# The up projection of a transformer layer by Strassen's seven block products, in a phase of its own

## The chip, the core and the metric

The kernel runs on one core of one Trainium2 chip. A core has TensorE (PE, matmuls into PSUM; PEld is its weight load), VectorE (DVE), ScalarE (ACT), GpSimd (POOL) and SyncE (SP), which here issues every DMA. The metric is the device time of one execution in microseconds, as the median of several runs; lower is better.

## The reference: what is computed

One layer of a hybrid backbone over 1024 latent tokens and 128 context tokens, in float32. A mixer (bidirectional mLSTM and attention) comes first, then a feed-forward block with a normalisation behind it. Only the second half matters here:

```python
x = layer_norm(ALPHA * x + g1 * mix, ln1_g, ln1_b)
h = x * (1 + sc2) + sh2
ff = jnp.square(jax.nn.relu(h @ w_up)) @ w_down
x = layer_norm(ALPHA * x + g2 * ff, ln2_g, ln2_b)
```

`h` is 1152 x 1024 (both token groups together), `w_up` 1024 x 4096, `w_down` 4096 x 1024.

## The kernel before, in words

Float32 products are made of three matmuls. `split` (L69) writes a rounded copy `hi` (ScalarE) and the rest `lo = src - hi` (VectorE); `mm3` (L73) issues hi x hi, hi x lo and lo x hi into one PSUM bank. Every operand of a large matmul goes through `split` first.

The work runs in four stages: projections and mLSTM, attention, branch projections with merge and output projection, feed-forward. Tokens stand in nine groups of 128 (`NT`), three of which make a block of 384 (`TB`, `NTB` = 3). A scheduler of the compiler sets the order on each engine from the program's order and the dependencies; engines take their rows strictly in that order and wait by semaphores. Buffers come from pools with a tag and a number of copies; a tile waits until its copy is free.

At the end of stage 3, for each token group, the output projection (`g3`) is followed by residual, `layer_norm` (VectorE statistics, GpSimd for the root and the gain, VectorE for the bias), a store of `x1` to DRAM, and `modulate2`: eight transposes on TensorE, eight scale-and-shift steps (four on VectorE, four on ScalarE), and a split into `h2T`, which stays in SBUF. The last group's `modulate2` is issued from within the first up block (the `mid` argument of `up`).

The feed-forward takes 16 blocks of 256 hidden units (`NFB`). `up(fb)` (L1111) multiplies a block of `w_up` with all tokens: three token blocks, two halves of the hidden units, eight steps of the contraction, three matmuls each, 144 of 384 columns. ScalarE's Relu, VectorE's square and a split follow. `down(fb)` (L1131) adds the block's share of the output: nine token groups, two halves of the columns, two steps, three matmuls, 108 of 512 columns; VectorE adds each result to `acc` (L1143). The loop puts `up(fb + 1)` ahead of `down(fb)`. The last two blocks go down together (`last`), with the final residual and `finish` (second normalisation and output) behind each group. `residual(s)` (L1158) adds the gate and `x1` to `acc`; it is spread over the last `up`, its `x1` tile has one buffer.

## Time and profile before

| quantity | value |
|---|---|
| median of 3 runs | 2476.15 us (2475.36 to 2480.89) |
| profiled execution, first to last instruction | 2469.1 us |
| feed-forward, from the first up matmul (1651.5) to the end | 817.6 us |
| TensorE busy, share of the span | 97% |
| VectorE, ScalarE, GpSimd busy | 57%, 34%, 13% |
| mean granted TensorE clock | 0.990 |
| moved by DMA | 264.8 MB, 107 GB/s |

The profile has the span of the profiled execution, not what lies around it; the median is 7.05 us above the span. In rows of groups stand the line, the engine, the operation, output and inputs by the program's names, the shape and the count, then busy time and the mean of one in ns, then the idle time before and what ended it. In rows in order of time stand the start, the length, the engine, the line, the names, and in brackets an idle time before with what ended it. A matmul's recorded length overlaps its neighbours'. In the view of stretches, each engine's busy time and count stand in the order PE, PEld, DVE, ACT, POOL, then clock, DMA share and GB/s.

### The profile page before, as it was taken

The numbers are of one execution on the slowest core, as the hardware profiler recorded it, in microseconds if no ns is written. First come the engines' busy times: TensorE is split into PE (matmuls) and PEld (weight loads), VectorE is DVE, ScalarE is ACT, GpSimd is POOL, SyncE is SP. The second block draws the span as 40 slices with busy tenths as digits, with TensorE's granted clock in tenths as the row PEclk, the third lists the DMA queues.
The fourth block names the chain that finished last, engine by engine and source line by source line (L and its number), as shares of the span: only waits on it lengthen the run. The fifth ranks groups of instructions, "written<-read, shape, count | busy, mean of one in ns | idle before, by whom it ended". The sixth has DMA issues, their size and how long they took to land. (4 is left out here: it accounts for less than half of the span.)

```text
span 2469.1 us, 35511 instructions
## 1 busy us (share of the span) xinstructions
PE 2387.7 (97%) x13485; PEld 2163.7 (88%) x13485; DVE 1399.7 (57%) x2625; ACT 843.8 (34%) x1844; POOL 312.3 (13%) x514
## 2 busy tenths in 40 slices
PE   6999998999999899899999999999999999999997
PEld 4888887788899899889999999888999899989985
DVE  5645635645654464378787345674445444544488
ACT  3323423534433243266666333132221122212221
POOL 1001100211110010134442000230000000000004
PEclk9999999999999999999999999999999999999998
DMA  7264447445654642520001655241111111111131
GB/s 266 87 206 152 148 120 198 138 125 146 196 165 145 183 148 95 104 72 17 16 16 58 216 188 189 93 141 35 52 35 52 35 52 35 51 35 52 35 120 77
DMA packets 211162, 264.77 MB, mean 107 GB/s; under 512 B 23760, under 2 KB 157984, under 8 KB 210992
## 3 DMA queue, kind: packets, MB, share of 16 engines
q1 hardware_dynamic: 210992, 262.51, 34.7%
q8 instruction: 106, 1.74, 0.3%
q14 instruction: 64, 0.52, 0.1%
HBM read 197.23 MB, written 65.21 MB: 106 GB/s over the span
## 5 line engine op out<-in xcount | busy, mean ns | idle before, releaser
L76 PE MATMUL g<-th,wh 128*128 128x384 f32 x1088 | 373.5, 343 | 8.7 <-DVE fm L246 8.7
L78 PE MATMUL g<-th,wl 128*128 128x384 f32 x1088 | 368.3, 338 | 0.0
L77 PE MATMUL g<-tl,wh 128*128 128x384 f32 x1088 | 366.7, 337 | 0.0
L70 ACT ACTIVATE wh<-raw 128x1024 fp32r<-128x1024 f32 x148 | 154.9, 1058 | 405.8 <-PE d L78 289.4
L76 PE MATMUL u<-th,wh 128*128 128x384 f32 x768 | 256.8, 335 | 0.8 <-ACT th L70 0.8
L77 PE MATMUL u<-tl,wh 128*128 128x384 f32 x768 | 256.7, 334 | 0.6 <-DVE tl L71 0.6
L78 PE MATMUL u<-th,wl 128*128 128x384 f32 x768 | 256.7, 334 | 0.0
L76 PE MATMUL g<-wh,th 128*128 128x512 f32 x600 | 241.1, 402 | 0.0
L77 PE MATMUL g<-wl,th 128*128 128x512 f32 x600 | 236.1, 394 | 0.7 <-DVE wl L71 0.7
L78 PE MATMUL g<-wh,tl 128*128 128x512 f32 x600 | 236.5, 394 | 0.0
L1143 DVE TENSOR_TENSOR acc<-acc,d 128x512 f32<-128x512 f32 x234 | 159.4, 687 | 119.6 <-PE d L78 119.6
L77 PE MATMUL d<-wl,ah 128*128 128x512 f32 x576 | 224.6, 390 | 2.3 <-DVE wl L71 2.3
L76 PE MATMUL d<-wh,ah 128*128 128x512 f32 x576 | 224.4, 390 | 1.8 <-DVE r L1146 1.6
L78 PE MATMUL d<-wh,al 128*128 128x512 f32 x576 | 224.4, 390 | 0.0
L76 PEld LDWEIGHTS g<-th,wh 128*128 128x128 f32 x1088 | 206.3, 190 | 17.5 <-DVE fm L246 9.0
L71 DVE TENSOR_TENSOR wl<-raw,wh 128x1024 fp32r<-128x1024 f32 x148 | 180.8, 1230 | 71.2 <-ACT wh L70 70.6
L78 PEld LDWEIGHTS g<-th,wl 128*128 128x128 f32 x1088 | 206.1, 189 | 0.4 <-issue 0.4
L77 PEld LDWEIGHTS g<-tl,wh 128*128 128x128 f32 x1088 | 206.4, 190 | 0.1
L1123 DVE TENSOR_TENSOR r<-r 128x384 f32<-128x384 f32 x96 | 53.5, 558 | 166.4 <-ACT r L1122 166.3
L76 PEld LDWEIGHTS u<-th,wh 128*128 128x128 f32 x768 | 144.1, 188 | 1.7 <-ACT th L70 1.1
L77 PEld LDWEIGHTS u<-tl,wh 128*128 128x128 f32 x768 | 144.2, 188 | 1.5 <-DVE tl L71 1.0
L78 PEld LDWEIGHTS u<-th,wl 128*128 128x128 f32 x768 | 144.1, 188 | 0.0
(307 smaller groups left out, 4675.4 us busy)
## 6 DMA issues: line engine op xcount, KB each, us to landing
raw<-in_w_in_dram SPq DMA_DIRECT2D x44, 512.0 KB
kvt<-kvd SPq DMA_DIRECT2D x64, 257.0 KB
raw<-in_w_mod_dram SPq DMA_DIRECT2D x32, 512.0 KB
raw<-in_w_up_dram SPq DMA_DIRECT2D x32, 512.0 KB
raw<-in_w_down_dram SPq DMA_DIRECT2D x32, 512.0 KB
kvd<-kvs SPq DMA_DIRECT2D x36, 257.0 KB
uw<-ud SPq DMA_DIRECT2D x72, 128.0 KB
bs<-st SPq DMA_DIRECT2D x32, 258.0 KB
```

What stands on the lines that cost most here:

```text
L70: nc.scalar.activation(out=hi, in_=src, func=AF.Copy)
L71: nc.vector.tensor_tensor(out=lo, in0=src, in1=f(hi), op=ALU.subtract)
L76: nc.tensor.matmul(out, lhsT=ah, rhs=bh, start=start and i == 0, stop=False)
L77: nc.tensor.matmul(out, lhsT=ah, rhs=bl, start=False, stop=False)
L78: nc.tensor.matmul(out, lhsT=al, rhs=bh, start=False, stop=stop and i == n - 1)
L1123: nc.vector.tensor_tensor(out=r, in0=r, in1=r, op=ALU.mult)
L1143: nc.vector.tensor_tensor(out=acc[:, s, cs], in0=acc[:, s, cs], in1=g[:], op=ALU.add)
```

## The change

The up projection is computed by Strassen's scheme (in Winograd's form) on 2 x 2 blocks: the contraction is halved into 512 and 512, the hidden units of a block into 128 and 128, and the tokens of a part into two halves. Two parts (`SUB`): 512 tokens with halves of 256, and 640 with halves of 320. Each of the seven products is four contraction steps of three matmuls, 12 matmuls of 256 or 320 columns, 84 per part and block. The activation operands (`act_forms`: four sums and differences, seven splits per part) are made once and stay; the weight operands are made for every block (`up_forms`: four combinations on GpSimd, L1177, and seven splits). The products add up in three PSUM tiles per part (`x`, `y`, `z`), and `evac` combines them by VectorE, with relu and square, into `ao`, which is stored to DRAM (`ffd`).

So that it fits, the feed-forward is two phases. `modulate2` stores `h2` to DRAM (`h2d`) in place of splitting it; the pools of the stages before are closed; the first four entries of `up_run` take block 0 and 1 for part 0, then 0 and 1 for part 1, with `act_forms` spread over them; the other 14 take both parts in turn. Then the up phase's pools are closed, and the down phase loads each block's activations from `ffd`, splits them and its weights (`down_load`), and multiplies as before. `residual` for all groups is issued after block 13's `down`.

```diff
+SUB = ((0, 256), (512, 320))
     def modulate2(s):
-        if s % 3 == 0:
-            h2T.append(t_alloc())
         hf = dt_([128, KT, 128], "m", 8)
         modulate(hf, s, x1s[s], sc2p, 24, t3)
-        o = (s % 3) * 128
-        split(h2T[s // 3][0][:, :, o:o + 128], h2T[s // 3][1][:, :, o:o + 128], hf[:])
+        store(h2d[s][:], hf[:])
...
+    modulate2(NS)
     st3.close()
+    stw.close()
+    st3r.close()
...
+    ORDER = ("a11", "s2", "a12", "s3", "s1", "a22", "s4")
...
+    def act_forms(i, pieces):
...
+        form("a11", b11)
+        t1 = ft([128, 4, 320], "bt")[:, :, 0:n]
+        sub(t1, b12, b11)
+        sub(b11, b22, t1)
+        form("s2", b11)
+        yield
+        form("a12", b21)
+        yield
+        sub(b12, b22, b12)
+        form("s3", b12)
+        yield
+        form("s1", t1)
+        yield
+        sub(b11, b21, b11)
+        form("a22", b11)
+        yield
+        form("s4", b22)
+        yield
...
+    def up_forms(raw):
...
+        def comb(tag, x, y, op):
+            t = ft([128, 4, 128], tag)
+            nc.gpsimd.tensor_tensor(out=t[:], in0=x, in1=y, op=op)
+            return t[:]
+
+        def form(src):
+            hi, lo = ft([128, 4, 128], "uh", 3, F32R), ft([128, 4, 128], "ul", 3, F32R)
+            split(hi[:], lo[:], src)
+            return hi, lo
...
+    def evac(st, j, fb, i):
...
+        if j == 0:
+            nc.scalar.activation(out=u("u1"), in_=X[:], func=AF.Copy)
+            st["a"] = ft([128, 2, 640], "ao", 2)[:, :, 0:2 * n]
+        elif j == 1:
+            tsum(u("u2"), st["u1"][:], Y[:])
...
+            nc.vector.scalar_tensor_tensor(out=dst, in0=dst, scalar=0.0, in1=dst, op0=ALU.max, op1=ALU.mult)
+            if j == 6:
+                store(ffd[fb][i][:], st["a"])
...
+            for j, nm in enumerate(ORDER):
+                for i in subs:
...
+                    for k in range(4):
+                        for a_, b_ in ((wh, bh), (wh, bl), (wl, bh)):
+                            nc.tensor.matmul(o, lhsT=a_[:, k, :], rhs=b_[:, k, :], start=first,
+                                             stop=k == 3 and b_ is bh and a_ is wl, skip_group_check=True)
...
+    up_run([(0, (0,), hook0), (1, (0,), None), (0, (1,), hook1), (1, (1,), None)] + [(fb, (0, 1), None) for fb in range(2, NFB)])
+    st4.close()
...
+    def down_load(fb):
+        ws = []
+        ar = et([128, 2, 1152], "ar", 2)
...
+            load(ar[:, :, o:o + 2 * n], ffd[fb][i][:])
...
+            ah, al = et([128, 1152], "ah", 5, F32R), et([128, 1152], "al", 5, F32R)
+            split(ah[:], al[:], ar[:, m, :])
+            wh, wl = et([128, D], "wh", 5, F32R), et([128, D], "wl", 5, F32R)
+            split(wh[:], wl[:], raw[:])
...
+    nxt = down_load(0)
     for fb in range(NFB - 2):
-        nxt = up(fb + 1)
-        down([fb], [a], False)
-        a = nxt
+        cur, nxt = nxt, down_load(fb + 1)
+        down(cur, fb == 0, False)
...
+    for s in range(NT):
+        residual(s)
+    down(nxt + down_load(NFB - 1), False, True)
```

How the rows of an engine's queue move is shown at three places. The first is SP's queue at the change of stage; `x1d` and `h2d` are the DRAM copies of a token group's normalised and modulated values, `raw` and `ur` weight tiles, `b00` to `b11` the four quarters of part 0's activations. Before, the first weights of the up projection (`in_w_up`) stood ahead of the first group's store:

```order
L64 DMA raw_16908<-in_w_out_dram 128x2x512
L64 DMA raw_16914<-in_w_out_dram 128x2x512
L64 DMA raw_17740<-in_w_up_dram 128x4x256
L64 DMA raw_17746<-in_w_up_dram 128x4x256
L64 DMA m_16996<-in_x_sample_dram 128x1024
L67 DMA x1d0_268<-m_16926 128x1024
```

Now:

```order
L70 DMA h2d7_284<-m_17738 128x1024
L70 DMA x1d8_276<-m_17668 128x1024
L70 DMA h2d8_285<-m_17758 128x1024
L67 DMA b00_17792<-h2d0_277 128x4x128
L67 DMA b00_17792<-h2d1_278 128x4x128
L67 DMA b01_17795<-h2d2_279 128x4x128
L67 DMA b01_17795<-h2d3_280 128x4x128
L67 DMA b10_17798<-h2d0_277 128x4x128
L67 DMA b10_17798<-h2d1_278 128x4x128
L67 DMA b11_17801<-h2d2_279 128x4x128
L67 DMA b11_17801<-h2d3_280 128x4x128
L67 DMA ur_17819<-in_w_up_dram 128x4x256
```

The first up weights moved from before the last groups' stores to the ninth place behind the last of them.

The second place is VectorE's queue in the first up block (`r` and `al` were its squares and splits; `fa110l` and the like are the low parts of part 0's activation operands, `ul` those of the weights, `u2` a sum of products). Before:

```order
L1123 TENSOR_TENSOR r_17890<-r_17890 128x384
L71 TENSOR_TENSOR al_17753<-r_17890,ah_17752 128x384
L1123 TENSOR_TENSOR r_17920<-r_17920 128x384
L71 TENSOR_TENSOR al_17753<-r_17920,ah_17752 128x384
L71 TENSOR_TENSOR wl_18158<-raw_18155,wh_18157 128x1024
```

Now:

```order
L74 TENSOR_TENSOR fs20l_17812<-b00_17792,fs20h_17811 128x1024
L74 TENSOR_TENSOR fs30l_17850<-b01_17795,fs30h_17849 128x1024
L74 TENSOR_TENSOR ul_17834<-s2_17825,uh_17833 128x512
L74 TENSOR_TENSOR ul_17840<-ur_17821,uh_17839 128x512
L74 TENSOR_TENSOR ul_17869<-s3_17831,uh_17868 128x512
L74 TENSOR_TENSOR fs10l_17874<-bt_17808,fs10h_17873 128x1024
L1201 TENSOR_TENSOR u2_0_17889<-u1_0_17865,y_17872 128x256
L74 TENSOR_TENSOR ul_17892<-s1_17823,uh_17891 128x512
L1140 TENSOR_TENSOR b00_17792<-b10_17798,b00_17792 128x4x256
L74 TENSOR_TENSOR ul_17915<-ur_17821,uh_17914 128x512
```

The activations' operands stand among the weights' and the sums, ahead of what the later products of the same entry need.

The third place is VectorE's queue ahead of the last phase (`acc` the running output, `x1` the reloaded residual; `r` at L1123 the squares of the last up block, at L1146 before and L1329 now the first evacuation of the last phase). Before:

```order
L71 TENSOR_TENSOR al_22874<-r_23018,ah_22873 128x384
L1168 SCALAR_TENSOR_TENSOR acc_17960<-x1_23027,acc_17960 128x1024
L1123 TENSOR_TENSOR r_23056<-r_23056 128x384
L71 TENSOR_TENSOR al_22874<-r_23056,ah_22873 128x384
L71 TENSOR_TENSOR wl_23113<-raw_23110,wh_23112 128x1024
L1168 SCALAR_TENSOR_TENSOR acc_17960<-x1_23061,acc_17960 128x1024
L71 TENSOR_TENSOR wl_23119<-raw_23116,wh_23118 128x1024
```

Now:

```order
L1351 SCALAR_TENSOR_TENSOR acc_21878<-x1_24260,acc_21878 128x1024
L1350 TENSOR_TENSOR acc_21878<-acc_21878,g20_24244 128x1024 x2
L1350 TENSOR_TENSOR acc_21878<-acc_21878,g21_24246 128x1024
L74 TENSOR_TENSOR al_24290<-ar_24284,ah_24289 128x1152
L1351 SCALAR_TENSOR_TENSOR acc_21878<-x1_24264,acc_21878 128x1024
L74 TENSOR_TENSOR wl_24294<-dw_24287,wh_24293 128x1024
L74 TENSOR_TENSOR al_24300<-ar_24284,ah_24299 128x1152
L74 TENSOR_TENSOR wl_24304<-dw_24297,wh_24303 128x1024
L1351 SCALAR_TENSOR_TENSOR acc_21878<-x1_24268,acc_21878 128x1024
L1329 TENSOR_TENSOR r_24321<-d4_24308,g20_24244 128x512
```

The residual steps moved from between the squares of the last up block to between block 13's evacuations and the last phase, with block 15's splits among them; three of them come later still.

More of the change, by code (lines that the diff above doesn't have):

```diff
@@ L1130, in down, with act_load @@
[L1130 to L1131 removed]
+    ORDER = ("a11", "s2", "a12", "s3", "s1", "a22", "s4")
+    acts = {}
+    def act_load(i):
+        o, n = SUB[i]
+        out = []
+        for kh in range(2):
+            for th in range(2):
+                t = ft([128, 4, 320], f"b{kh}{th}")[:, :, 0:n]
+                c = o + th * n
+                while c < o + th * n + n:
+                    w = min(128 - c % 128, o + th * n + n - c)
+                    load(t[:, :, c - o - th * n:c - o - th * n + w], h2d[c // 128][:, 4 * kh:4 * kh + 4, c % 128:c % 128 + w])
+                    c += w
+                out.append(t)
+        return out
@@ new lines, in hybrid_step_kernel, with up_load @@
+    wuv = kview(w_up)
+    def up_load(fb):
+        out = []
+        for kh in range(2):
+            t = ft([128, 4, 256], "ur", 3)
+            load(t[:], wuv[:, 4 * kh:4 * kh + 4, 256 * fb:256 * fb + 256])
+            out.append(t)
+        return out
+    def up_forms(raw):
+        a11, a21 = raw[0][:, :, 0:128], raw[0][:, :, 128:256]
+        a12, a22 = raw[1][:, :, 0:128], raw[1][:, :, 128:256]
+        def comb(tag, x, y, op):
[4 more added lines that the diff above has]
+            hi, lo = ft([128, 4, 128], "uh", 3, F32R), ft([128, 4, 128], "ul", 3, F32R)
+            split(hi[:], lo[:], src)
+            return hi, lo
+        s1 = comb("s1", a21, a22, ALU.add)
+        s2 = comb("s2", s1, a11, ALU.subtract)
+        yield form(a11)
+        s3 = comb("s3", a11, a21, ALU.subtract)
+        yield form(s2)
+        s4 = comb("s4", a12, s2, ALU.subtract)
+        yield form(a12)
+        yield form(s3)
+        yield form(s1)
+        yield form(a22)
+        yield form(s4)
@@ L1132, in down @@
+    def down(ws, first, last):
         for s in range(NT):
```

157 lines of the change are left out of this document (103 added, 54 removed).

## The prediction

> **What bounds the kernel now.** I read the page's head and slices first, then the stretches of 100 us over the feed-forward, then single matmuls in order of time.
>
> ```profile
> span 2469.1 us, 35511 instructions
> PE 2387.7 (97%) x13485; PEld 2163.7 (88%) x13485; DVE 1399.7 (57%) x2625; ACT 843.8 (34%) x1844; POOL 312.3 (13%) x514
> ```
>
> ```profile
> 1700.00:1800.00 100.00, 100.00 (x511) 91.50 (x510) 46.95 (x68) 20.68 (x33) 0.00 (x0) 1.00 0.14 43
> 2300.00:2400.00 100.00, 99.45 (x506) 90.44 (x504) 64.31 (x85) 19.81 (x33) 0.00 (x0) 1.00 0.28 95
> ```
>
> The columns of the second view are stretch, PE, PEld, DVE, ACT and POOL busy, clock, DMA share, GB/s. TensorE never rests in the feed-forward, at full clock; VectorE is half idle, GpSimd empty. So a saving in matmul time counts here, and so does every wait that the change opens on TensorE. What one matmul costs is its start-to-start distance, not its recorded length (matmuls overlap):
>
> ```profile
> 1439.94 0.33 PE L76 MATMUL g<-th,wh 128*128 128x384 f32 x1
> 1459.87 0.33 PE L77 MATMUL g<-xl,wh 128*128 128x384 f32 x1
> ...
> 1704.46 0.39 PE L76 MATMUL d<-wh,ah 128*128 128x512 f32 x1
> 1728.76 0.39 PE L78 MATMUL d<-wh,al 128*128 128x512 f32 x1
> ...
> 1344.13 0.28 PE L76 MATMUL pv<-ph,vh 128*128 128x256 f32 x1
> 1346.74 0.28 PE L78 MATMUL pv<-ph,vl 128*128 128x256 f32 x1
> ```
>
> Between the rows lie 115, 107 and 23 steps: 0.1733 us for 384 columns, 0.227 for 512, 0.1135 for 256. A block of 256 hidden units costs 16 x 9 = 144 matmuls of 384 columns up, 24.96 us, and 108 of 512 down, 24.5 us.
>
> **What the change saves.** Up, a block is now seven products of 12 matmuls for each token part, 84 of 256 columns and 84 of 320. No row has 320: between the rows of 256 and 384, by length, it is 0.1435 us; its ends are 0.140 (the 256 row's excess of 7 ns over 256 columns at the 0.417 ns per column between 384 and 512) and 0.147 (the 384 row's excess of 13 ns). A block takes 84 x (0.1135 + 0.1435) = 21.6, with a little at the starts 21.7 us (21.3 to 22.0). Over 16 blocks that saves 16 x 3.26 = 52 us. Is a steady block still TensorE's? VectorE's steps:
>
> ```profile
> 2379.62 2.36 DVE L71 TENSOR_TENSOR wl<-raw,wh 128x1024 fp32r<-128x1024 f32 x2
> 1664.32 1.02 DVE L1123 TENSOR_TENSOR r<-r 128x384 f32<-128x384 f32 x2
> L1181 POOL TENSOR_TENSOR acc<-acc,l 128x1024 f32<-128x1024 f32 x8 | 20.6, 2572 | 16.7 <-DVE acc L1180 14.5 <-PE d L78 2.1
> ```
>
> The second of two adds 1.14 us at 1024 and 0.46 at 384; by that line 512 takes 0.6, 1280 1.41, 256 and 320 0.33 and 0.40. A block has seven weight splits of 512 (4.2), ten sums of the products, five a part (3.7), and four squares of 256 to 640 (2.1): 10 us of 21.7. GpSimd's four combinations of 512 (L1177) are half of the L1181 row each, 1.2 us (the eight of that row have 2.57 at 1024, 2.40 where nothing came between, below), 4.8 us together. Even one after the other the two engines fit. A weight operand has three buffers, so it can be made as soon as the product three before it has ended, and is needed two products (6.2 us) later; ScalarE's half and VectorE's half of it take 1.2 us together. So I take no stall in the 14 steady blocks: 14 x 21.7 = 304 us. What I cost at nothing besides: the activations' way through DRAM, 1.2 MB out in a block up, 1.2 MB and 1 MB of weights in a block down, lies beside 21.7 and 24.5 us of matmuls; at the 371 GB/s of a row below 2.2 MB are 6 us, with 3 fixed, and if that cover were gone each down block would pay these 9. ScalarE's squares of the first product (two of 256 and 320) lie beside the same matmuls, since it is 21% busy in the 1700 row.
>
> **What it adds: four places where TensorE waits.** First, the start. Before, the last row group's normalisation ran beside the first up matmuls:
>
> ```profile
> 1651.55 0.42 PE L76 MATMUL u<-th,wh 128*128 128x384 f32 x1
> ...
> 1652.71 0.68 DVE L1091 TENSOR_TENSOR m<-g,m 128x512 f32<-128x512 f32 x1
> 1657.79 0.81 DVE L1056 TENSOR_SCALAR m<-m,bmv,brs 128x1024 f32<-128x1024 f32 x1 [0.72 <-POOL brs L1048]
> 1662.04 1.23 DVE L1058 TENSOR_TENSOR m<-m 128x1024 f32<-128x1024 f32 x1 [2.30 <-POOL m L1057]
> ...
> 1658.74 3.26 POOL L1057 TENSOR_TENSOR m<-m 128x1024 f32<-128x1024 f32 x1 [0.98 <-issue]
> ...
> 1654.99 1.49 ACT L197 ACTIVATE m<-t,modT,sc2p 128x128 f32<-128x128 f32 x4
> ```
>
> Now all loads of the new phase stand on SP's queue behind the store of that last group, though the first part needs only groups 0 to 3: eight loads of activations and three of weights are queued there, ScalarE's first split waits for the first of them, VectorE for ScalarE, TensorE for both. The chain ended at 1663.3; it loses two weight splits (2.1) and GpSimd's wait beside a third (0.85), so 1660.3. Transposes (1.0), four L197-like steps (1.5) and the issue bring the first load to 1663.3. Ahead of the first weights lie 1 MB of stores and 2.1 MB of loads, then 0.5 MB:
>
> ```profile
> 9.00:11.00 2.00, 1.87 (x8) 0.14 (x8) 0.00 (x0) 0.00 (x0) 0.00 (x0) 1.00 1.06 371
> 30.00:34.00 4.00, 3.01 (x11) 2.69 (x9) 0.69 (x1) 0.63 (x1) 0.00 (x0) 0.68 1.04 412
> 34.00:38.00 4.00, 2.80 (x20) 2.12 (x20) 3.23 (x9) 1.71 (x3) 0.00 (x0) 1.00 1.03 386
> ```
>
> At 371 GB/s 3.6 MB take 9.7 us, so weights at about 1673, split at 1673.7: 22.2 us without up matmuls (18 if the stores are through earlier, 27 with a slower transfer).
>
> Second, the ramp, the first four entries of the new loop (blocks 0 and 1, each part alone), 43.2 us of TensorE work. VectorE must make all activation operands in it: 12 steps of 1.14 us for part 0 and 12 of 1.41 for part 1. When the first product starts five of part 0's are through; before the third entry's last operand come 8.0 + 16.9 + 21 weight splits (12.6) + evacuations (2 x 2.6 and 0.8) = 43.5 us, then two products (3.4) and the fourth entry (12.1): 59 us, the ramp ends at 1732.7. GpSimd's 12 combinations of these entries add up to 14.4 us, if they shut VectorE out:
>
> ```profile
> 2418.84 2.40 POOL L1181 TENSOR_TENSOR acc<-acc,l 128x1024 f32<-128x1024 f32 x1 [2.31 <-DVE acc L1180]
> ...
> 2409.62 0.69 DVE L1147 TENSOR_TENSOR acc<-acc,r 128x512 f32<-128x512 f32 x1
> 2419.40 2.39 DVE L1147 TENSOR_TENSOR acc<-acc,r 128x512 f32<-128x512 f32 x1
> 2418.68 0.68 DVE L1146 TENSOR_TENSOR r<-d,g 128x512 f32<-128x512 f32 x1
> ```
>
> The same sum of 512 takes 0.69 us alone and 2.39 beside GpSimd, ending just after it; one with a PSUM operand took its usual 0.68. The ramp's splits all read SBUF twice, so I lean to the upper end, 1747, and take 1745: 71.3 us. The Trainium skill, "SBUF — State Buffer", section "Who interferes with whom", says that a two-SBUF-input VectorE operation and a GpSimd operation that reads SBUF take one port pair in turn, the later waiting in full. By that rule the ramp ends at 1747, without it at 1733; the L1147 rows agree with it.
>
> Third, the handover. The first loads of the down phase stand on SP behind the last store and need the up phase's memory. Two 320-wide evacuations (1.0), then a store and 1.2 MB of activations. What a load costs beyond its bytes:
>
> ```profile
> 2390.09 1.22 DVE L1168 SCALAR_TENSOR_TENSOR acc<-x,acc 128x1024 f32<-128x1024 f32 x1 [2.53 <-DMA x<-x1d]
> 2395.69 1.23 DVE L1168 SCALAR_TENSOR_TENSOR acc<-x,acc 128x1024 f32<-128x1024 f32 x1 [2.75 <-DMA x<-x1d]
> ```
>
> From the end of the one (2391.3) to the start of the other lies one reload of 0.5 MB: 4.4 us, 1.4 of it bytes, 3.0 fixed. So 1.0 + 3.0 + 3.1, then ScalarE's three splits (3.4) and one subtraction (1.3) before the second matmul, 12 us; the clock falls in such a pause (0.68 over 30 to 34 us in the row above, where matmuls came after idling), about 1.5 us more: 13.5 (10 to 17).
>
> Fourth, the end. The down blocks stay 24.5 us, 14 of them 342.7. The residuals, once beside the last up block, now run with block 13 and after it: after block 13's last evacuation VectorE's queue has six steps of them (6.8), the two pairs of splits of block 15 (4.8) and a wait for the single x1 buffer (about 1: a reload of 4.4 us against the 3.6 of steps between) before the first of the last 18 evacuations, 12.6 us after block 13. Behind that wait stand the evacuations, and behind the splits TensorE, whose last phase sums blocks 14 and 15 in one bank: it gets through six matmuls and stops. Three more (3.7 us) fall within the last phase, which is VectorE's already:
>
> ```profile
> 2403.68 0.69 DVE L1146 TENSOR_TENSOR r<-d,g 128x512 f32<-128x512 f32 x1 [0.35 <-PE d L78]
> ...
> 2464.57 1.29 DVE L1181 TENSOR_TENSOR acc<-acc,l 128x512 f32<-128x512 f32 x2
> ```
>
> From 2403.68 to the span's end are 65.4 us; now 69.1.
>
> **The sum.** 1651.5 + 22.2 = 1673.7; + 71.3 = 1745.0; + 304 = 2049; + 13.5 + 342.7 = 2405.2; + 12.6 + 69.1 = 2486.9, against the span of 2469.1. The median of the runs, 2476.15, is 7.05 above that span; I leave this as it is: **2494 us**, 0.7% slower. The saving of 52 is spent on start, ramp excess (28), handover and end.
>
> **Rivals.** A, faster: the splits keep pace and TensorE sets the ramp, 43.2 instead of 71.3: 2465.7. Below 48.7 us of ramp the change is a gain. Its idle half on VectorE speaks for it, the sum of 43.5 us before the third entry's last operand, without any wait, against it. B, no change: narrow matmuls lose their fixed part. At the bare 0.417 ns per column of the 384 and 512 rows, 256 and 320 columns take 0.107 and 0.133 us, a block 20.2, the 14 steady ones 21 us less: 2473. The 256 row of 0.1135 speaks against. The Trainium skill, "TensorE: Matmul & The Clock Gate", section "Back-to-back issue gap", has a rule near it, columns over 2.4 GHz plus 2.5 ns. By that rule 512 columns take 0.216 us, and the trace, 0.227, does not follow it; with it the forecast would be about 2479. C, slower: GpSimd's turn lands on an operand that TensorE waits for in each steady block, 1.2 us x 14: 2510.6. The 6 us of lead speak against. D, slower: with pauses between its products TensorE stays at half clock through the ramp's fourth entry too, 12 us more: 2506. The 0.68 row speaks for it, the next row, with the clock at 1.00 though TensorE was busy in 2.8 of 4 us, against it. E, the products are not cheaper in time, each as long as one of 384 columns: 14 x 7.4 = 104 us more, 2598; the 256 row excludes nearly all of it.
>
> **How the numbers follow.** My forecast has 0.57, with its own range 2480 to 2506 (ramp 1733 to 1749, start, handover and end by their ends); A 0.08, B 0.10, C 0.12, D 0.11, E 0.02. The range of 2472 to 2514 leaves out A and E and a tail on either side. A measurement tells 0.2%, 5 us, from no change: below 2471.2 lies A and a thread of the forecast's low tail, 0.11; to 2481.1 B and a part of that tail, 0.13; above it 0.76.
>
> **What would show it.** In the changed profile the first up matmul stands about 1674, the steady blocks at 21.7 us with TensorE full, the down phase's first matmul about 13 us after the last product, and a pause after its fourteenth block. A ramp under 50 us, or steady blocks over 22.5 us, would make the working wrong; a start before 1665 would mean that the queue order did not hold.

## The result, and the profile after

The changed kernel takes 2514.11 us (median of 4 runs, 2513.26 to 2515.53) against 2475.76 of the kernel before in the same comparison (2471.35 to 2480.89): 1.0153 times as long, with a 95% interval of 1.0139 to 1.0167, or 38.4 us. Slower, as forecast, but by twice the 18 us that were forecast, and 0.1 us above the range's upper end. The profiled execution has a span of 2511.4 us, and its own time is 2513.26.

Page of the changed kernel, its head:

```profile
span 2511.4 us, 37272 instructions
PE 2366.3 (94%) x13869; PEld 2136.4 (85%) x13869; DVE 1525.5 (61%) x2796; ACT 868.4 (35%) x1879; POOL 409.5 (16%) x586
```

Against before, TensorE is busy for 21.4 us less in a span that is 42.3 us longer, and VectorE for 125.8 us more. The time went into waits of TensorE. Where they lie is read from single rows in order of time: the last matmul of the output projection, the first of the up phase, the start of its fifth entry (block 2), a steady block, the last of the up phase, and the stops of the down phase.

```profile
1653.91 0.40 PE L81 MATMUL g<-wh,tl 128*128 128x512 f32 x1
1680.27 0.58 PE L1260 MATMUL x<-fa110h,uh 128*128 128x256 f32 x1 [15.33 <-ACT uh L73]
1754.16 0.28 PE L1260 MATMUL x<-fa110h,uh 128*128 128x256 f32 x1
...
1821.36 0.28 PE L1260 MATMUL x<-fa110h,uh 128*128 128x256 f32 x1
1822.79 0.31 PE L1260 MATMUL x<-fa111h,uh 128*128 128x320 f32 x1
1824.56 0.28 PE L1260 MATMUL y<-fs20h,uh 128*128 128x256 f32 x1
1843.76 0.28 PE L1260 MATMUL x<-fa110h,uh 128*128 128x256 f32 x1
...
2067.61 0.31 PE L1260 MATMUL z<-fs41h,ul 128*128 128x320 f32 x1
2079.14 1.22 PE L79 MATMUL d<-wh,ah 128*128 128x512 f32 x2 [11.22 <-ACT wh L73]
2089.67 0.50 PE L79 MATMUL d<-wh,ah 128*128 128x512 f32 x1 [1.63 <-DVE acc L1324]
2434.75 0.80 PE L80 MATMUL d<-wl,ah 128*128 128x512 f32 x1 [2.51 <-DVE wl L74]
```

Twelve matmuls of 256 columns go from 1821.36 to 1822.79, twelve of 320 from there to 1824.56: 0.1192 and 0.1475 us each, and a block takes 1843.76 - 1821.36 = 22.40 us. TensorE is full in these blocks; the stretches of the changed kernel show where it is not (columns as before: PE, PEld, DVE, ACT, POOL, clock, DMA share, GB/s).

```profile
1670.00:1680.00 10.00, 0.00 (x0) 0.00 (x0) 5.01 (x5) 4.42 (x5) 0.31 (x1) 0.50 1.07 305
1680.00:1690.00 10.00, 5.32 (x19) 4.43 (x20) 10.00 (x8) 4.04 (x7) 8.01 (x4) 0.50 0.35 104
...
1710.00:1720.00 10.00, 7.89 (x46) 7.18 (x45) 10.00 (x13) 5.91 (x8) 4.89 (x3) 0.83 0.32 89
1720.00:1730.00 10.00, 4.95 (x25) 3.85 (x25) 9.96 (x9) 3.79 (x7) 6.53 (x3) 0.89 0.25 91
...
1800.00:1900.00 100.00, 100.00 (x752) 100.00 (x751) 50.44 (x92) 31.13 (x61) 24.64 (x19) 1.00 0.29 102
```

The first four entries, from 1680.27 to 1754.16, are the ramp; they take 23.0, 14.2, 24.4 and 12.3 us. In the first three VectorE is the full engine and TensorE the one that waits. The fourth already goes at the pace of its matmuls, at clock 1.00, with VectorE busy for 9.7 of 12.3 us. In the steady blocks TensorE is full, with VectorE at half.

The stages ahead of the feed-forward do nearly the same work in the kernel before, the changed one and the experiments (the changed ones store `h2` in place of splitting it), and still the output projection's last matmul stands between 1648.0 and 1655.7 us from one execution to the next (1650.53 in the kernel before). So the experiments are compared from that matmul on, each by its one profiled execution, beside the ratio of the medians. The first two columns are called the start and the ramp from here on, the fourth the tail:

| us from the last output projection matmul | to the first up matmul | ramp, to block 2 | one steady up block | last up matmul to the end | the whole |
|---|---|---|---|---|---|
| before | 1.0 | - | 24.96 | - | 818.6 |
| after | 26.4 | 73.9 | 22.40 | 443.8 | 857.5 |

For the changed kernel 26.4 + 73.9 + 14 x 22.40 + 443.8 make the 857.5, within the rounding: 38.9 more than before, close to the 38.4 between the medians.

### The profile page after: what moved, and what is told of

Its sections match the earlier page's. It is cut to its first block, busy times and chain, and to the rows that moved or that the text cites. A ratio compares the mean times of both kernels' runs of the same rounds, so it can differ in the third digit from the quotient of the medians.

```text
span 2511.4 us, 37272 instructions
## 1 busy us (share of the span) xinstructions
PE 2366.3 (94%) x13869; PEld 2136.4 (85%) x13869; DVE 1525.5 (61%) x2796; ACT 868.4 (35%) x1879; POOL 409.5 (16%) x586
## 5 line engine op out<-in xcount | busy, mean ns | idle before, releaser
L79 PE MATMUL d<-wh,ah 128*128 128x512 f32 x576 | 225.4, 393 | 18.2 <-ACT wh L73 11.2
L79 PEld LDWEIGHTS d<-wh,ah 128*128 128x128 f32 x576 | 109.0, 189 | 43.0 <-ACT wh L73 11.5
L73 ACT ACTIVATE ah<-ar 128x1152 fp32r<-128x1152 f32 x32 | 36.9, 1158 | 299.2 <-PE d L80 278.4
L79 PEld LDWEIGHTS g<-wh,th 128*128 128x128 f32 x600 | 113.2, 189 | 26.3 <-issue 3.8
L74 DVE TENSOR_TENSOR wl<-raw,wh 128x1024 fp32r<-128x1024 f32 x84 | 103.8, 1237 | 49.2 <-ACT wh L73 48.5
L81 PEld LDWEIGHTS g<-wh,tl 128*128 128x128 f32 x600 | 113.0, 188 | 23.5
L80 PEld LDWEIGHTS g<-wl,th 128*128 128x128 f32 x600 | 113.1, 189 | 21.4 <-DVE wl L74 1.8
L80 PEld LDWEIGHTS d<-wl,ah 128*128 128x128 f32 x576 | 108.8, 189 | 25.9 <-DVE wl L74 3.6
L81 PEld LDWEIGHTS d<-wh,al 128*128 128x128 f32 x576 | 108.9, 189 | 22.7
L73 ACT ACTIVATE wh<-raw 128x1024 fp32r<-128x1024 f32 x84 | 88.6, 1058 | 94.8 <-PE g L80 44.0
```

The source lines that it names most:

```text
L73: nc.scalar.activation(out=hi, in_=src, func=AF.Copy)
L74: nc.vector.tensor_tensor(out=lo, in0=src, in1=f(hi), op=ALU.subtract)
L79: nc.tensor.matmul(out, lhsT=ah, rhs=bh, start=start and i == 0, stop=False)
L80: nc.tensor.matmul(out, lhsT=ah, rhs=bl, start=False, stop=False)
L81: nc.tensor.matmul(out, lhsT=al, rhs=bh, start=False, stop=stop and i == n - 1)
```

## The experiments

My theory after the result: the forecast's four pauses are all there, and together somewhat longer than worked out; the ramp is set by VectorE, which GpSimd shuts out; and the largest error is the price of a narrow matmul, 4 to 6 ns too low in each of 2688. The rivals: a stall in every steady block, the low clock as the cause of the ramp, the memory's placement as the cause of the dearer matmuls, and, for the change as a whole, that the two phases through DRAM cost it and not Strassen's forms.

**GpSimd's sums on VectorE.** The weights' four combinations of each block move to the engine that they shut out.

```diff
-            nc.gpsimd.tensor_tensor(out=t[:], in0=x, in1=y, op=op)
+            nc.vector.tensor_tensor(out=t[:], in0=x, in1=y, op=op)
```

> The changed kernel with the four weight combinations of each block (L1177) on VectorE in place of GpSimd, nothing else. In the changed kernel VectorE's steps in the ramp that stood beside a GpSimd combination were about 1 us longer than their like, 16 us in all, and the ramp took 73.9 us. Theory 1 (VectorE's own queue with the shared port sets the ramp): the 16 us go, 16 combinations of 0.6 us come, 9.6 us: the ramp takes about 68 us, the steady blocks stay at 22.4 us since TensorE sets them, and the time is about 2508 us. Theory 2 (the longer steps lay in time that VectorE waited anyway; loads, the lower clock and the chain from ScalarE to VectorE set the ramp): the ramp stays at 74 or grows by up to 9.6 us, 2514 to 2524 us.

The ramp fell from 73.9 to 67.5 us, the whole from 857.5 to 851.5 us; ratio to before 1.0134 (1.0119 to 1.0149). VectorE got 16 sums of about 0.6 us more in the ramp, 9.6 us, and the ramp was still 6.4 us shorter: the shutting out had cost 16. The trace says the same: in the changed kernel's ramp VectorE's steps are longer than the shorter ones of their shape by 16.2 us in all, here by 0.3. The same kind of split, first in the changed kernel (beside it GpSimd's row), then in this one:

```profile
1684.76 2.28 DVE L74 TENSOR_TENSOR fs30l<-b,fs30h 128x1024 fp32r<-128x1024 f32 x1
1683.83 2.13 POOL L1177 TENSOR_TENSOR s<-s,ur 128x512 f32<-128x512 f32 x1
```

```profile
1688.57 1.22 DVE L74 TENSOR_TENSOR fs40l<-b,fs40h 128x1024 fp32r<-128x1024 f32 x1
```

2.28 us where GpSimd works and 1.21 where it doesn't, as the forecast took from the L1147 rows. The rule of the Trainium skill, "SBUF — State Buffer", section "Who interferes with whom", agrees with both. The steady block stayed at 22.40 us: there neither engine is the bound, so rival C (GpSimd's turn in each steady block) is excluded from this side too.

**The last groups' stores on another queue.** The stores of groups 7 and 8 are issued by GpSimd, so that SP's queue does not stand behind them.

```diff
-        store(h2d[s][:], hf[:])
+        (store if s < NS - 1 else late_st)(h2d[s][:], hf[:])    # late_st: nc.gpsimd.dma_start
-        store(x1d[s][:], xt[:])
+        (store if s < NS else late_st)(x1d[s][:], xt[:])
```

> The changed kernel with the last three stores ahead of the change of phase (h2 of groups 7 and 8, x1 of group 8) issued by GpSimd in place of SP, nothing else. Theory 1 (the loads of the new phase are late because they stand behind these stores on SP's queue): they are issued when the last output projection has freed its buffers, about 1656 us instead of 1666.9, the first up matmul stands about 1669 instead of 1680.3, and the time falls by 9 to 12 us, to about 2503. Theory 2 (the buffers come free only with the last normalisation and its modulation, about 1666 us): under 3 us of gain, 2511 to 2514.

The start fell from 26.4 to 21.8 us, the whole to 851.5, ratio 1.0129 (1.0112 to 1.0146). SP's queue, first in the changed kernel, then here:

```profile
1666.50 0.32 SPq L70 DMA_DIRECT2D h2d<-m  x1
1666.88 6.72 SPq L67 DMA_DIRECT2D b<-h2d  x8
```

```profile
1645.56 6.29 SPq L67 DMA_DIRECT2D b<-h2d  x8
```

In the changed kernel the eight loads wait for group 8's store although they need groups 0 to 3 only; here they are issued before it, 2.4 us ahead of the last output projection matmul (1647.96) instead of 13.0 behind. Of these 15.4 us only 4.5 arrive, because TensorE waits for splits that now stand among group 8's normalisation on ScalarE and VectorE:

```profile
1661.53 3.45 DVE L77 TENSOR_TENSOR fa110l<-b,fa110h 128x1024 fp32r<-128x1024 f32 x1 [1.97 <-ACT fa110h L76]
1669.13 0.61 ACT L76 ACTIVATE uh<-ur 128x512 fp32r<-128x512 f32 x1
```

The first split runs at 1661.5, beside GpSimd and so for 3.45 us; the first product waits for a weight's rounding at 1669.1. What was late next, once the queue was clear, was the two engines that share the normalisation.

**The ramp over four blocks.** Part 0 of blocks 0 to 3, then part 1 of the same four, with part 1's operands spread over three entries.

```diff
-    up_run([(0, (0,), hook0), (1, (0,), None), (0, (1,), hook1), (1, (1,), None)] + [(fb, (0, 1), None) for fb in range(2, NFB)])
+    up_run([(0, (0,), hook0)] + [(fb, (0,), hook1) for fb in (1, 2, 3)] + [(fb, (1,), None) for fb in range(4)] + [(fb, (0, 1), None) for fb in range(4, NFB)])
```

> The changed kernel with four blocks of part 0, then four of part 1 ahead of the joint ones, part 1's operands (act_forms) spread over three entries; weights of blocks 2 and 3 are so formed twice. Theory 1 (in the ramp VectorE has more to do than TensorE; given more matmuls beside it, it no longer stops TensorE): first entry 23 us as now, the other seven near their matmul time, 3 x 10.0 + 4 x 12.4 = 79.6, so 103 us for four blocks instead of 73.9 + 2 x 22.4 = 118.7, and 2498 us. Theory 2 (a single part's products, 1.4 us each, are too short for the chain from weight to split, so every entry of part 0 alone loses some 4 us): 2507 to 2514 us.

Nothing: four blocks took 119.5 us, against 73.9 + 2 x 22.4 = 118.7; the whole 857.8, ratio 1.0160 (1.0145 to 1.0176). The four entries of part 0, then the four of part 1:

```profile
1677.19:1747.30 70.11, 53.84 (x336) 50.34 (x337) 67.84 (x72) 32.53 (x51) 36.05 (x20) 0.80 0.41 126
1747.30:1796.71 49.41, 49.41 (x339) 49.29 (x337) 40.82 (x59) 22.22 (x40) 22.99 (x17) 1.00 0.41 138
```

Part 0's entries took 23.9, 18.3, 16.9 and 11.0 us for 10.0 of matmuls each, with VectorE full; part 1's took 12.3 to 12.5, which is their matmul time, with VectorE busy for 83%. So neither theory is right. An entry does not lose 4 us for being of one part alone: part 1's lose nothing, and part 0's last, with hardly any operands left to make, loses 1.0. But an entry of part 0 has next to no room for operands either: its weights' splits and its evacuations take VectorE about 9 us (8.90 of 11.35 us in its second entry of the last run below, which makes no operands) beside the 10.0. The room there is, some 2 us in each entry of part 1, comes when all operands have been made.

**The up phase's memory from the other side.** The up phase's pool is laid from the other end of the memory, to see whether the dearer matmul comes from where the operands lie.

```diff
-    fp = pool(st4, "fp", 1)
+    fp = pool(st4, "fp", 1, side="right")
```

> The changed kernel with the up phase's pool laid from the upper end of the memory downwards, so that its tiles lie at other addresses; nothing else. It asks why 256 columns take 0.1195 us start to start in the up phase and 0.1135 in attention, whose operands lie at the upper end. Theory 1 (the place of the operands): 0.1135 us now, a block 21.9 instead of 22.4 us, 7 us less in all. Theory 2 (the matmul's own fixed part, as for 320, 384 and 512 columns): 0.1195 and 22.4 us as before.

In a single execution the whole took 859.3 us, a block again 22.40, twelve matmuls of 256 and of 320 columns again 1.44 and 1.77:

```profile
1780.52 0.28 PE L1260 MATMUL x<-fa110h,uh 128*128 128x256 f32 x1
1781.96 0.31 PE L1260 MATMUL x<-fa111h,uh 128*128 128x320 f32 x1
...
1802.92 0.28 PE L1260 MATMUL x<-fa110h,uh 128*128 128x256 f32 x1
```

The price does not come from the place, at least not between these two. It is what the kernel before pays in another stage, too: 18 matmuls of 258 columns from 188.55 to 190.72, 0.1206 us each.

```profile
188.55 0.28 PE L76 MATMUL op<-vh,sh 128*128 128x258 f32 x1
...
190.72 0.40 PE L76 MATMUL g<-wh,th 128*128 128x512 f32 x1
```

**Two phases without Strassen.** The old up projection for all 16 blocks, its result through DRAM, then the changed kernel's down phase.

```diff
-    up_run([(0, (0,), hook0), ...])
+    for fb in range(NFB):
+        up(fb, (lambda: modulate2(NS)) if fb == 0 else None)    # three blocks of 384 columns; r is stored to ffd[fb]
```

> Only the half of the change that makes two phases: the up projection as before (three blocks of 384 tokens, 144 matmuls of 384 columns a block, h2T split in SBUF, the last group's modulation inside the first up block), but all 16 blocks first, their outputs stored to DRAM, then the down phase of the changed kernel. It separates the price of the phases from Strassen's. By the sum of what the changed profile shows: first up matmul within 2 us of the last output projection; 16 x 24.96 = 399.4 us up; then, as in the changed kernel, 11.4 us to the first down matmul and 432.3 us from there to the end: 843 us from the first up matmul against 817.6 before, so 25 us more than before, a ratio of 1.010. Then Strassen's seven products, with 16 x 2.56 = 41 us of matmul time saved, cost a further 13 us net in the changed kernel by start (26 us) and ramp (29 us more than its matmuls). Rival: the phases cost next to nothing by themselves (under 8 us, ratio under 1.003), and nearly the whole loss is Strassen's.

The whole is 847.1 us, 28.5 more than before; ratio 1.0123 (1.0108 to 1.0138). Its matmuls in order of time:

```profile
2054.09 0.34 PE L81 MATMUL u<-th,wl 128*128 128x384 f32 x1
2064.71 2.08 PE L79 MATMUL d<-wh,ah 128*128 128x512 f32 x4 [10.29 <-ACT wh L73]
2076.22 0.79 PE L79 MATMUL d<-wh,ah 128*128 128x512 f32 x1 [2.23 <-DVE acc L1167]
```

There is no ramp, and the first up matmul stands 1.0 us behind the output projection. The phases alone cost 10.6 us of pause at the handover, 6.4 of further stops and half clock (0.50 from 2060 to 2069) in the first down block, 14.3 at the end (85.8 us from the last two blocks' first down matmul, at 2413.87, to the end of the span, against 71.6 before) and 1.1 in the up blocks. The kernel before loses 3.9 us of its own between its blocks, 3.0 of it in the first two up blocks; with these off, 28.5. Strassen's forms on top of this cost 857.5 - 847.1 = 10.4 more. They save 16 x (24.96 - 22.40) = 41 us and pay 25.4 at the start (26.4 for 1.0) and 73.9 - 2 x 22.4 = 29.1 in the ramp; 13.5 of loss, of which 1.1 for the plain up blocks and 1.8 for a shorter tail go off.

**The first down inputs early.** Block 0's activations and weights of the down phase are loaded during the last up entry, into the memory of the quarters `b00` to `b11`, for which the quarters get a pool of their own.

```diff
-                t = ft([128, 4, 320], f"b{kh}{th}")[:, :, 0:n]
+                t = bt_([128, 4, 320], f"b{kh}{th}")[:, :, 0:n]    # pool "bp"
...
+            if n == len(jobs) - 1:
+                pre_load()    # ffd[0] and w_down's first two tiles into the quarters
```

> The changed kernel with the first down block's activations and weights loaded during the last up block, into the tiles that held the activations' quarters; splits as before, in the down phase. Theory 1 (the pause at the handover is the loads behind the last store on SP's queue): the splits find their buffers free before the last products end, the first down matmul follows the last up matmul in 1 to 3 us instead of 11.5, the clock does not fall, the stall of 1.6 us behind it goes, and the time falls by 10 to 12 us. Theory 2 (the buffers for the split operands come free only with the last products): the splits, 4.5 us, stand in the pause, 6 us instead of 11.5, and 5 to 6 us of gain.

The whole is 849.4 us, ratio 1.0118 (1.0103 to 1.0133). At the handover the pause of 11.2 us became short ones, of 2.82 us and less:

```profile
1667.61 0.58 PE L1267 MATMUL x<-fa110h,uh 128*128 128x256 f32 x1 [7.33 <-ACT uh L73]
...
2057.79 0.31 PE L1267 MATMUL z<-fs41h,ul 128*128 128x320 f32 x1
2061.61 0.50 PE L80 MATMUL d<-wl,ah 128*128 128x512 f32 x1 [2.82 <-DVE wl L74]
```

The tail gained 2.9 us (440.9), 4.2 at the handover less 1.3 given back at the end. Another 8.0 us I had not planned: they fell at the start, which took 18.35 instead of 26.4. Against that the ramp took 76.7 instead of 73.9; that may be no effect of the edit, for the run with the other placement has 76.5, and the two-block ramps of all runs that leave the sums on GpSimd and the operands in place lie between 72.9 and 76.7. That makes the 8.1 of the whole, where 10 to 12 were expected from the handover alone. With a pool of their own the quarters' memory was free earlier, so the scheduler issued their loads between the last groups' stores (the last at 1658.60) and only the weights behind group 8's:

```profile
1658.60 0.43 SPq L67 DMA_DIRECT2D b<-h2d  x1
1661.85 0.33 SPq L70 DMA_DIRECT2D h2d<-m  x1
1662.22 2.11 SPq L67 DMA_DIRECT2D ur<-in_w_up_dram  x3
```

That is a second witness for the queue's order as the cause of the long start.

**The last bias on VectorE.** In the last phase the final addition of `finish` moves from GpSimd to VectorE for every group, not only the last.

```diff
-            (nc.gpsimd if s < NS else nc.vector).tensor_tensor(out=y, in0=y, in1=l2b[:, cs], op=ALU.add)
+            nc.vector.tensor_tensor(out=y, in0=y, in1=l2b[:, cs], op=ALU.add)
```

> The changed kernel with the last step of each of the first eight groups (L1364, adding the bias of the second normalisation) on VectorE in place of GpSimd; nothing else. In the last phase VectorE is busy 66.9 of 70 us, and its sums of two SBUF operands (L1330) end 2.2 us late beside each GpSimd step. Theory 1 (GpSimd's step shuts VectorE out for longer than VectorE would need for it): 7.24 us per group fall to about 6.2, 7 to 9 us less in all. Theory 2 (VectorE's own work is the bound, and one step of 1.2 us more per group is added): 7.24 stay or grow, 0 to 9 us more.

The tail fell from 443.8 to 435.4, the whole to 850.0, ratio 1.0135 (1.0118 to 1.0152). VectorE's queue in the changed kernel, two groups apart by 7.23 us, with GpSimd's bias between them, and then here, 5.64 and 6.83:

```profile
2458.86 1.28 DVE L1363 SCALAR_TENSOR_TENSOR acc<-acc,brs,l2g 128x1024 f32<-128x1024 f32 x1
2466.09 1.28 DVE L1363 SCALAR_TENSOR_TENSOR acc<-acc,brs,l2g 128x1024 f32<-128x1024 f32 x1
2467.29 0.68 DVE L1330 TENSOR_TENSOR acc<-acc,r 128x512 f32<-128x512 f32 x1
2467.46 2.78 POOL L1364 TENSOR_TENSOR acc<-acc,l2b 128x1024 f32<-128x1024 f32 x1 [0.99 <-DVE acc L1363]
2467.89 2.88 DVE L1330 TENSOR_TENSOR acc<-acc,r 128x512 f32<-128x512 f32 x1
```

```profile
2466.80 1.28 DVE L1363 SCALAR_TENSOR_TENSOR acc<-acc,brs,l2g 128x1024 f32<-128x1024 f32 x1
2471.66 0.68 DVE L1330 TENSOR_TENSOR acc<-acc,r 128x512 f32<-128x512 f32 x1
2472.44 1.28 DVE L1363 SCALAR_TENSOR_TENSOR acc<-acc,brs,l2g 128x1024 f32<-128x1024 f32 x1
2479.27 1.29 DVE L1363 SCALAR_TENSOR_TENSOR acc<-acc,brs,l2g 128x1024 f32<-128x1024 f32 x1
```

Of a group's two L1330 sums the one ahead of GpSimd's bias took 0.68 us and the one beside it 2.88; without GpSimd both take 0.68. So VectorE gains 2.2 us and takes over one sum of 1024, 1.2 us as elsewhere. About 1 us for each of eight groups makes the 8.4.

**Longer rows in DRAM.** `h2` is stored by quarters and each quarter lies without gaps in SBUF, so that it is one load with rows of 4 KB; before, the loads went in rows of 512 bytes.

```diff
-    h2d = [dr.tile([128, KT, 128], F32, name=f"h2d{s}") for s in range(NT)]
+    h2q = [[[dr.tile([128, 4, n], F32, name=f"h2q{i}{kh}{th}") for th in range(2)] for kh in range(2)] for i, (_, n) in enumerate(SUB)]
...
-                t = ft([128, 4, 320], f"b{kh}{th}")[:, :, 0:n]
...
+                t = ft([128, 1280], f"b{kh}{th}")[:, 0:4 * n].rearrange("p (k n) -> p k n", n=n)
+                load(t, h2q[i][kh][th][:])
```

> The changed kernel with h2 kept in DRAM by the quarters in which it is loaded (per part, half of the contraction, half of the tokens), so that each quarter is one load with rows of 4 KB in place of two loads with rows of 512 B; the stores are the shorter ones now. The loads before the first up matmul ran at 275 to 305 GB/s where the forecast had taken 371 from a stretch of weight loads. Theory 1 (short rows slow the loads): 3.6 MB at 371 GB/s, the first up matmul 2 to 3 us nearer to the last output projection than the 26.4 us of the changed kernel. Theory 2 (rows of 512 B cost nothing here): 26 us as before.

In a single execution the start took 23.9 instead of 26.4 us, the whole 853.9. Where nobody touched the start, it took 25.6 to 26.5. The loads of the activations moved 352 GB/s; in the changed kernel the row while they alone moved has 272, and the 305 above has the weights in it:

```profile
1666.00:1670.00 4.00, 0.00 (x0) 0.00 (x0) 0.00 (x0) 1.04 (x1) 0.00 (x0) 0.50 0.99 352
```

```profile
1668.00:1674.00 6.00, 0.00 (x0) 0.00 (x0) 1.23 (x1) 1.06 (x1) 0.00 (x0) 0.50 0.97 272
```

The DMA engines were equally full (0.99 and 0.97), so it was not the smaller number of loads that made the difference. The forecast's 371 GB/s nearly holds for longer rows; the short ones cost 2.5 us here.

**Four repairs together.** The sums and the last bias on VectorE, the late stores aside, the first down inputs early, and block 15's operands made ahead of the residuals (whose `x1` gets three buffers).

```diff
-        x1 = et([128, D], "x1")
+        x1 = et([128, D], "x1", 3)
...
+    nxt = nxt + down_load(NFB - 1)
     for s in range(NT):
         residual(s)
-    down(nxt + down_load(NFB - 1), False, True)
+    down(nxt, False, True)
```

> The changed kernel with four edits together: the weight combinations on VectorE (e1), the last three stores of the stage before issued by GpSimd (e2), the first down block's inputs loaded early (e6), the last bias on VectorE (e7); besides, block 15's operands ahead of the residual steps in program order and three x1 buffers. Measured from the last output projection's matmul to the end, the changed kernel takes 857.5 us, the kernel before 818.6, and the four edits gave 6.0, 6.0, 8.1 and 7.5 us. Theory 1 (they repair different places and add up): 829 us, 10 us over the kernel before, a ratio of about 1.004. Theory 2 (e1 and e2 both shorten the same queue of VectorE, so one of them gives nothing beside the other): 835 us, 1.007. Neither makes it faster than before, since ramp and start still cost some 45 us against 41 saved.

829.8 us, ratio 1.0048 (1.0031 to 1.0065). The sum came out, but not place by place: the start is 16.9, 9.5 less, where the two that shorten it had 4.5 and 8.0 alone, since both clear the same queue; the ramp is 68.7, the tail 430.8, 13.0 less. There the early inputs and the last bias had 2.9 and 8.4 alone; block 15's operands ahead of the residuals, which no run tries by themselves, are in the rest. So it is partly luck that the whole came within 1 us of the sum.

**The last bias in the kernel before.** The same edit as above, in the kernel before, whose last phase has the same lines.

```diff
-            (nc.gpsimd if s < NS else nc.vector).tensor_tensor(out=y, in0=y, in1=l2b[:, cs], op=ALU.add)
+            nc.vector.tensor_tensor(out=y, in0=y, in1=l2b[:, cs], op=ALU.add)
```

> The kernel before with the last bias (L1181) on VectorE in place of GpSimd, nothing else: the share of e7 that has nothing to do with the change. Theory (the shared port costs as much there): 5 to 8 us less than before, a ratio of 0.997 to 0.998. Rival (TensorE is closer to being the bound there, so nothing comes of it): 0.9995 to 1.001.

815.7 instead of 818.6 us, ratio 0.9985 (0.9974 to 0.9997). It is the only kernel of this study that is faster than before. The gain is 2.9 us of the 5 to 8 that I had expected, between the theory and its rival. The L1147 sums had lost less there: seven of the 18 were late beside GpSimd, by 0.7 to 1.7 us (the 2.39 of the prediction's row is such a one), 8.5 in all, against seven by 2.2 in the changed kernel, 15.3 in all. Eight biases on VectorE cost 9.7, more than these 8.5; where the 2.9 come from is not shown.

**The operands ahead of the phase.** Part 0's operands are made from group 4 of the stage before to its end, from SBUF, and the first weights are loaded there; part 1's are hooked into the second entry. The repairs stay, with two differences: the first down inputs go by GpSimd's queue in place of being loaded early, and the squares of the up projection move to ScalarE.

```diff
     def modulate2(s):
+        if s < 4:
...
+            modulate(Quarters(s), s, x1s[s], sc2p, 24, t3)    # into part 0's quarters in SBUF
+            return
...
+        if s == 4:
+            g0 = act_forms(0, c12[0][:, 0], c12[0][:, 1], c12[0][:, 2], c12[1], pair0)
+        if 4 <= s < NS:
+            next(g0)
+    for _ in range(3):
+        next(g0)
```

> The seven products with part 0's operands made while stage 3 still runs: groups 0 to 3 are modulated straight into SBUF, the sums and splits (act_forms) are issued between the last groups' normalisations into the buffers that the token blocks leave, the first weights are loaded then too; part 1's operands follow during the two entries of part 0. With it combinations, last bias on VectorE, all squares of the up projection on ScalarE, the first down block's inputs by GpSimd's queue, block 15's operands ahead of the residuals. If VectorE's work at the start of the phase is what the change pays with, moving 14 us of it beside stage 3's matmuls takes the start from 26 to about 13 us after the last output projection and the ramp from 74 to about 58; with 8 us at the handover and 8 at the end, 810 to 816 us from the last output projection to the end, against 818.6 before: a ratio of 0.993 to 0.999. Rival: the operands made in stage 3 delay its own normalisations by as much as they save later (stage 3 longer by 5 to 15 us), 1.000 to 1.006.

828.3 us, ratio 1.0041 (1.0027 to 1.0055): not to be told apart from the repairs alone, and short of what I had expected, which was no slower than before. The start took 16.1 us where I had expected 13, the ramp 64.5 for 58, and the handover, from the last up matmul to the second down block less a block's 24.5, 15.1 for 8. Three rows of VectorE with GpSimd's among them, then one of TensorE:

```profile
1659.61 1.22 DVE L78 TENSOR_TENSOR f<-c,f 128x1024 fp32r<-128x1024 f32 x1
1659.85 3.18 POOL L1067 TENSOR_TENSOR m<-m 128x1024 f32<-128x1024 f32 x1
1660.74 3.36 DVE L78 TENSOR_TENSOR f<-c,f 128x1024 fp32r<-128x1024 f32 x1
1664.03 1.21 DVE L1068 TENSOR_TENSOR m<-m 128x1024 f32<-128x1024 f32 x1
```

```profile
1707.40 0.64 PE L1316 MATMUL x<-fa11h,ul 128*128 128x320 f32 x1 [4.38 <-DVE ul L78]
```

Two early splits stand ahead of group 8's last normalisation step, which the start waits for. The second lies beside GpSimd's step of the same normalisation and takes 3.36 us in place of 1.22; the last step follows only then. In the ramp TensorE still stops for VectorE, here 4.38 us for a weight's split. The work had been moved to where VectorE's time was no cheaper.

**The ramp without VectorE's operand work.** The subtractions and low parts of `act_forms` are left out, so that this kernel does not compute the layer; the products, loads, weights and evacuations stay.

```diff
-            lo = ft([128, 4, n], f"f{nm}{i}l", 1, F32R)
-            split(hi[:], lo[:], src)
-            acts[nm, i] = (hi, lo)
+            nc.scalar.activation(out=hi[:], in_=src, func=AF.Copy)
+            acts[nm, i] = (hi, hi)
...
-            nc.vector.tensor_tensor(out=out, in0=x, in1=y, op=ALU.subtract)
+            pass
```

> The changed kernel with act_forms' whole VectorE work left out: the sums and differences of the activations aren't formed and the low parts aren't made (the high part stands in for them), so the up projection's values are not the layer's; every matmul, weight combination, split of weights, load and store stays. It measures what of the ramp is VectorE's work on these operands. Theory 1 (it sets the ramp): 24 steps, 30.6 us of VectorE, go, and with them most of the waits; the ramp falls from 73.9 us to about 50 (44.8 of matmuls, a few us at the lower clock), the start by 1 to 2 us, and the steady blocks stay at 22.4. Theory 2 (the ramp is set by the weights' chain, GpSimd to ScalarE to VectorE to TensorE, when a part runs alone): over 62 us.

In a single execution the ramp fell from 73.9 to 54.0 us (from the first matmul at 1670.24 to 1724.22), the start from 26.4 to 15.3, the whole to 827.2. The start's 11 us, where I had expected 1 to 2, cannot be put down to VectorE alone: the scheduler also issued five of the eight loads at 1652.5 here, ahead of the last output projection matmul, and earlier loads by themselves had shortened the start by 4.5 and 8.0, though not the ramp. The clock is full from 1686:

```profile
1686.00:1696.00 10.00, 9.59 (x80) 9.39 (x79) 6.95 (x12) 9.44 (x15) 4.60 (x4) 1.00 1.01 288
```

TensorE is nearly full again and VectorE is not. The ramp still is 9.2 us above two steady blocks, 8.0 of them in the first entry; its first 16 us go at a mean clock of 0.61. So VectorE's operand work sets the ramp, and costs 20 us there; the low clock of the changed kernel (0.50 to 1690, 0.83 and 0.89 in the rows to 1730) follows from the pauses rather than makes them. And it bounds what the change can reach: this start and ramp with the tail of the four repairs make 15.3 + 54.0 + 14 x 22.4 + 430.8 = 813.7 us, 5 below the kernel before, and that with the operands for nothing and their loads issued early.

## Why the prediction was wrong

The direction was right, slower with 0.76; the size was not. The step that failed is the first price, in "What the change saves": 0.1135 us for a matmul of 256 columns, taken from the pv row, and 0.1435 for 320, worked out from it. Measured are 0.1192 and 0.1475. The saving is 41 us and not 52. In the 14 steady blocks alone that is 9.5 of the 24.5 us by which the span is longer than forecast. 3.4 lie in the stages ahead, within what these differ by from one execution to the next; the other steps missed by 1.1 to 3.2 us. All went one way, but for the handover's pause, so nearly nothing cancelled within the span; outside it 4.3 us did, by luck:

| step of the sum | forecast | measured | difference |
|---|---|---|---|
| stages ahead, to the last output projection matmul | 1650.5 | 1653.9 | +3.4 |
| from there to the first up matmul | 23.2 | 26.4 | +3.2 |
| ramp | 71.3 | 73.9 | +2.6 |
| 14 steady up blocks | 304 | 313.5 | +9.5 |
| handover | 13.5 | 11.5 + 3.9 | +1.9 |
| 14 down blocks | 342.7 | 342.7 | 0 |
| to the last phase | 12.6 | 13.7 | +1.1 |
| last phase | 69.1 | 71.9 | +2.8 |
| span | 2486.9 | 2511.4 | +24.5 |
| around the span | 7.05 | 2.7 | -4.3 |

**The price of a matmul.** The forecast priced 384 and 512 columns from dozens of rows, and each had 13 ns over its 0.417 ns per column. It gave 256 columns only 7 ns, because one group of 24 rows (pv) said so. That was no stray reading: over all pv groups of that trace, 712 steps, the middle one is 0.115. The rows of 258 columns in the same trace (0.1206) would have said 13 ns again. With the fixed 13 ns the block is 84 x (0.1197 + 0.1463) = 22.3 us and the sum 9 us higher. The forecast had this end for 320 columns only, and took the one row of the new width for a better guide than the line through all others. Rival B, cheaper narrow matmuls, had it the wrong way round. The Trainium skill, "TensorE: Matmul & The Clock Gate", section "Back-to-back issue gap", has 2.5 ns there, for a matmul by itself; by an estimate from it 256 columns would take 0.109 us, and the trace, 0.119, does not follow. Why pv's matmuls go at 0.1135 stays open: only the placement was tried.

**The start.** The mechanism, loads behind the last group's store on one queue, is shown by the two runs that changed the order. The loads were issued 13.0 us behind the last output projection matmul, where the forecast had 12.8; from there to the first product it was 13.4 for 10.4. Of these 3.0 us longer rows give back 2.5, with 352 GB/s in place of 272; the forecast had 371.

**The ramp.** VectorE is the bound, and GpSimd shuts it out in full: 73.9 against a forecast of 71.3 to 73.3, shown by the run with the sums moved (16 us of waiting) and the run without the operands. Rival A, TensorE sets the ramp, is excluded. (The ramp below which the change would have been a gain is 53.5 us by the forecast's own sum, 71.3 less the 17.8 between 2494 and 2476.15, and not 48.7; no other figure hangs on it.) So is rival D as it was put, half clock through the fourth entry: that entry took 12.3 us at clock 1.00. The low clock is there in the rows of the first three, but VectorE sets the pace in them.

**The steady blocks.** No stall in them, TensorE 100.00 of 100; rival C is excluded. E needed no run: 22.40 us is not 29.

**Handover and end.** The pause of 11.5 was shorter than the forecast's 13.5, and 3.9 us of later stops and half clock (0.50 from 2073 to 2082) in the first down block, for which the 13.5 held 1.5, came on top. In the last phase the forecast kept the time of before's last phase and added three residual steps; it did not see that groups now come 7.23 us apart, with one of the two L1330 sums of each 2.2 us late beside GpSimd's bias. Something of that was to be had in either kernel: 8.4 us in the changed one, 2.9 in the one before.

**Around the span.** The 7.05 us between span and median were for the most part not a fixed piece: this execution has 1.9 us outside its span, and before's runs lie between 2471 and 2481. Two medians can be compared; a span plus the difference of a median from another execution's span carries that spread.

## What to carry to other kernels

Price a matmul of a new width from the line through every width in the trace, start to start, and where one kind of matmul falls off it, work out both prices before choosing; on 2688 matmuls 4 to 6 ns were 11 us. A change that cuts a projection's columns by an eighth must be charged with the phase it needs: here two phases in place of one cost 28.5 us alone, half of it at the end, and the loads and operands that Strassen's forms need before they can start another 54, start and ramp together, against 41 saved. Where VectorE is the bound of a stretch, look at what GpSimd does beside it: a sum on GpSimd can cost VectorE more than doing it itself.

## What the runs showed of the hardware

- **A fixed part per matmul.** At 256, 258, 320, 384 and 512 columns the distance of matmuls with a weight load each is 0.417 ns per column and about 13 ns (0.1192, 0.1206, 0.1475, 0.1733, 0.227 us), and moving the operands to the other end of the memory changed nothing. The pv matmuls at 256 columns, with 0.1135 to 0.115, are the exception, and it is not explained.
- **The clock after a pause.** Behind the pause of 15 us the granted clock was 0.50 to 1690 us, and then 0.83 to 0.89 in the rows of 10 us to 1730, as long as pauses went on (it was 1.00 and 0.50 by turns: 1.00 over 1694 to 1700, 0.50 over 1700.8 to 1704); without them, in the run without VectorE's operand work, it was 1.00 by 1686, 16 us after the first matmul.
- **Rows of 512 bytes.** The loads of the activations moved 272 GB/s with rows of 512 bytes and 352 with 4 KB, the DMA engines 0.97 and 0.99 busy.
- **Stages that were hardly changed** differed by 7.7 us between executions (1648.0 to 1655.7 for the same matmul), which is why differences of a few us were taken from that matmul on.
